# A hybrid attention and state-space layer on one core: a planner's rule for GpSimd, and another order of the first tiles

## The chip, the core and the metric

The kernel runs on one core of one Trainium2 chip. Its engines work side by side and wait for each other through semaphores: TensorE (PE, with its weight loads PEld), VectorE (DVE), ScalarE (ACT), GpSimd (POOL) and SyncE (SP), which issues most of the DMAs. The metric is device microseconds of one execution, and less is better.

## The reference, cut to what matters

`x` is 1024 tokens by 2048, all in float32. One combined projection gives ten blocks of columns; two mixers work on them, and one output projection with a residual and a LayerNorm ends the layer.

```python
u = jnp.einsum('bsd,de->bse', h, w_in[layer])              # 2048 -> 6752 columns
q, k, v, z_attn, q_idx, k_idx, w_idx, z_ssd, xbc, dt_raw = _split_cols(u, IN_WIDTHS)
# group A: indexer scores  sum_h w_idx * relu(q_idx . k_idx)  with 16 heads, the top 256 admissible
#   keys of each query, softmax attention over them (8 query heads, 2 key heads), times silu(z_attn)
o_attn = _dsa_attention(q, k, v, q_idx, k_idx, w_idx) * jax.nn.silu(z_attn)
# group B: causal conv of 4 taps and silu on xbc, chunked state-space scan in 4 groups,
#   gated RMSNorm with silu(z_ssd)
o_ssd = _ssd_mixer(xbc, z_ssd, dt_raw, conv_w[layer], conv_b[layer], ...)
mixed = jnp.concatenate([o_attn, o_ssd], axis=-1)
sub = jnp.einsum('bse,ed->bsd', mixed, w_out[layer])
h = _layer_norm(DEEPNORM_ALPHA * h + sub, ln_g[layer], ln_b[layer])
```

## The kernel before, in words

**Projection.** The tokens are worked on in two halves (`h` = 0 and 1) of 512. The columns are cut into 53 tiles of 128 (`ORDER`): `qi` are the eight tiles of indexer queries, `misc` holds indexer keys, indexer weights and dt, `xbc` and `zs` feed the state-space mixer, `k`, `v`, `q`, `z` the attention. A tile needs all 16 blocks of 128 rows of the weights (`KT` = 16); these come in two pieces (`u` = 0 and 1) of 128x1024 floats, 512 KB each. Every float32 operand is split into a high and a low part of type fp32r: ScalarE copies the high part (`wh` from `wr`, `xh` from the raw tokens), and VectorE or GpSimd subtracts it from the raw value to get the low part (`wl`, `xl`). One block then takes three matmuls: `wh` with `xh`, `wh` with `xl`, `wl` with `xh` (`emit_t`). In half 0 a `qi` tile uses only the upper 256 of the 512 tokens, since the lower 256 have no more admissible keys than the top 256.

**Output projection.** 64 more weight pieces (`O`) follow in the same stream and the same split, with four row blocks of tokens each; LayerNorm ends it.

**What sets the order.** The program is written out by a planner while it is built. `Flow` keeps a list of tasks (generators such as `t_qi`, `t_xbc`, `t_ssd`, `t_attn`, `t_topk`), each of which says what it needs; `Sim` holds a model of every engine's clock, and `pump` emits a task's next step when the model says that its inputs are there. Between the tasks the main loop of `run` emits the matmuls of the stream, four steps (`q`) of two blocks a piece; weights are loaded up to eight pieces ahead and split two ahead (`WAHEAD`). On the chip each engine runs its own instructions in the order in which they were emitted. Because all instructions are recorded by one helper, nearly all carry one line in the profile, L290, and are told apart by the names of their tiles.

**GpSimd or VectorE.** `Sim` has a model of a port that the two engines share (`Port`, `shares_port`): where both want it, one of them waits. `pick` chooses an engine for the low part of a weight piece or of the tokens; everywhere else the engine stands in the code ("V" or "G").

**The opening before.** Nine matmuls on zeros (`warm_up`), then the first weight piece in two DMAs, the upper 256 columns of all 16 token blocks in eight DMAs, and the first four `qi` tiles; `misc` follows as the fifth tile. The lower 256 token columns are loaded and split during the third to seventh piece.

## Time and profile before

| | |
|---|---|
| time, median of 3 runs | 1815.16 us (1812.81 to 1815.38) |
| profiled execution: its own time | 1813.86 us |
| profiled execution: span of the trace | 1812.0 us |
| busy: PE / DVE / ACT / POOL | 98% / 57% / 51% / 26% |
| instructions: PE / DVE / ACT / POOL | 8709 / 1934 / 1571 / 415 |
| granted TensorE clock, mean | 0.994 |

The span runs from the first to the last instruction; the profiled execution's time is 1.86 us longer. Times within the trace are us from the start of the span. A PE that is called busy need not be at its peak: its matmuls overlap, and what counts is the distance from one start to the next.

### The profile page before, as it was taken

The page shows a single profiled execution, that of the slowest core. Times are in us where ns is not written, and L with a number is a line of the kernel's source. Part 1 is how long each engine was busy: PE and PEld are TensorE (multiplying, and loading weights), DVE is VectorE, ACT ScalarE, POOL GpSimd, SP SyncE. Part 2 cuts the span into 40 slices and gives each one's busy share as a digit, 9 for nine tenths or more (in the row PEclk, how much of TensorE's full clock was granted, in tenths as well). Part 3 has the DMA queues.
Part 4 walks back from the last instruction along what each step waited for, and adds up shares of the span by engine and source line. Part 5 has one row for each costly group of instructions (what it writes and reads, how often), then busy time and mean ns, then how long its engine had stood idle before and what let it go on. Part 6 is the DMA issues. An engine that isn't in the chain of part 4 may idle for free. (4 is left out here: it accounts for less than half of the span.)

```text
span 1812.0 us, 24251 instructions
## 1 busy us (share of the span) xinstructions
PE 1768.7 (98%) x8709; PEld 1474.0 (81%) x8709; DVE 1032.4 (57%) x1934; ACT 915.2 (51%) x1571; POOL 464.3 (26%) x415
## 2 busy tenths in 40 slices
PE   9999999999999999999999999999999999999996
PEld 7878888888888878878887888778888888888885
DVE  7855565555325567766755473465546445547435
ACT  6557673433234555566577768773365333431221
POOL 5310231121213133421212132022322122332123
PEclk9999999999999999999999999999999999999998
DMA  8323334333344542222333333333344344558642
GB/s 275 115 82 105 109 111 126 111 128 120 134 146 131 192 137 76 76 67 70 99 105 109 119 111 122 117 122 140 120 155 156 110 144 131 158 173 278 222 163 93
DMA packets 120424, 238.11 MB, mean 131 GB/s; under 512 B 12784, under 2 KB 50928, under 8 KB 120304
## 3 DMA queue, kind: packets, MB, share of 16 engines
q1 hardware_dynamic: 120304, 236.57, 40.2%
q8 instruction: 68, 1.11, 0.2%
q14 instruction: 52, 0.43, 0.1%
HBM read 204.47 MB, written 32.05 MB: 131 GB/s over the span
## 5 line engine op out<-in xcount | busy, mean ns | idle before, releaser
L290 PE MATMUL pj<-xh,wh 128*128 128x512 f32 (+1 forms) x1696 | 665.0, 392 | 1.8 <-ACT xh L290 1.8
L290 PE MATMUL pj<-xh,wl 128*128 128x512 f32 (+1 forms) x1696 | 650.4, 383 | 0.6 <-DVE wl L290 0.6
L290 PE MATMUL pj<-xl,wh 128*128 128x512 f32 (+1 forms) x1696 | 650.0, 383 | 1.0 <-DVE xl L290 0.5
L290 DVE TENSOR_TENSOR wl<-wr,wh 128x1024 fp32r<-128x1024 f32 (+1 forms) x214 | 270.8, 1265 | 504.9 <-ACT wh L290 478.1
L290 ACT ACTIVATE wh<-wr 128x1024 fp32r<-128x1024 f32 (+1 forms) x272 | 283.8, 1045 | 272.9 <-PE pj L290 218.9
L290 PEld LDWEIGHTS pj<-xh,wl 128*128 128x128 f32 x1696 | 320.3, 189 | 64.8 <-DVE wl L290 1.2
L290 PEld LDWEIGHTS pj<-xh,wh 128*128 128x128 f32 x1696 | 320.7, 189 | 62.0 <-issue 2.9
L290 PEld LDWEIGHTS pj<-xl,wh 128*128 128x128 f32 x1696 | 320.9, 189 | 58.4 <-DVE xl L290 0.9
L290 POOL TENSOR_TENSOR u<-u,u 128x512 f32<-128x512 f32 (+8 forms) x164 | 177.1, 1092 | 509.5 <-DVE u L290 317.5
L290 POOL TENSOR_TENSOR wl<-wr,wh 128x1024 fp32r<-128x1024 f32 (+1 forms) x58 | 139.7, 2408 | 370.6 <-ACT wh L290 359.4
L290 PE MATMUL a<-u,u 128*128 128x512 f32 (+3 forms) x840 | 181.2, 342 | 8.9 <-DVE u L290 5.3
L290 PE MATMUL pj<-wh,xh 128*128 128x512 f32 x464 | 183.1, 395 | 0.7 <-ACT u L290 0.7
L290 PE MATMUL pj<-wl,xh 128*128 128x512 f32 x464 | 180.9, 390 | 0.0
L290 PE MATMUL pj<-wh,xl 128*128 128x512 f32 x464 | 180.8, 390 | 0.0
L290 PEld LDWEIGHTS a<-u,u 128*128 128x128 f32 x840 | 137.4, 189 | 40.9 <-DVE u L290 8.4
L290 ACT ACTIVATE u<-s,sm 128x640 bf16<-128x640 int16 (+7 forms) x132 | 130.1, 985 | 32.4 <-DVE sm L290 29.3
L290 ACT ACTIVATE u<-a 128x256 fp32r<-128x256 f32 (+3 forms) x182 | 61.7, 367 | 153.6 <-PE a L290 98.0
L290 ACT ACTIVATE u<-pj 128x512 f32<-128x512 f32 x90 | 53.4, 594 | 146.8 <-PE pj L290 127.4
L290 ACT ACTIVATE a<-a 128x512 f32<-128x512 f32 (+3 forms) x160 | 75.6, 505 | 80.5 <-PE a L290 76.2
L290 PEld LDWEIGHTS pj<-wh,xl 128*128 128x128 f32 x464 | 87.1, 188 | 18.6
L290 PEld LDWEIGHTS pj<-wh,xh 128*128 128x128 f32 x464 | 87.2, 188 | 17.6 <-ACT u L290 1.2
L290 PEld LDWEIGHTS pj<-wl,xh 128*128 128x128 f32 x464 | 87.3, 188 | 16.3
(120 smaller groups left out, 1758.2 us busy)
## 6 DMA issues: line engine op xcount, KB each, us to landing
wr<-wt SPq DMA_DIRECT2D x211, 512.0 KB, 3.3
wr<-wo SPq DMA_DIRECT2D x61, 512.0 KB, 3.7
s<-arow SPq DMA_DIRECT2D x32, 256.0 KB, 4.6
u<-mx SPq DMA_DIRECT2D x32, 256.0 KB, 4.9
u<-xn SPq DMA_DIRECT2D x32, 256.0 KB, 5.6
out<-u SPq DMA_DIRECT2D x32, 256.0 KB, 2.9
u<-arow SPq DMA_DIRECT2D x64, 64.0 KB, 4.3
mx<-u SPq DMA_DIRECT2D x16, 256.0 KB, 2.4
```

Source lines behind the costliest of these rows:

```text
L290: f(*args, **kw)
```

## The change

Three things. The choice between VectorE and GpSimd is made by the planner in more places (`two` calls `pick` where "G" stood in the code: the rope's sine product, the low parts of keys, values, queries and indexer queries, the state-space products), and `pick` has another rule: VectorE takes the operation if the model has it on the port at any time between GpSimd's start and end, and GpSimd takes it only if it would end first. The model's rule on which VectorE operations use the port is changed at small sizes. And the opening is another: `misc` and two `xbc` tiles (512 columns each) come first and take turns, two token blocks each; their first weight pieces come in three parts of 256, 256 and 512 columns; the first part of each is issued by ScalarE, all others by SP; the tokens come in whole blocks of 512 columns. 16 matmuls on zeros stand ahead in place of 9. An unused path (`KEEP`) is removed.

```diff
+FIRST = [("misc", 0), ("xbc", (0, 0)), ("xbc", (0, 1))]
+ORDERS = [[ORDER.index(x) for x in FIRST + [y for y in ORDER if y not in FIRST]],
+          [ORDER.index(x) for x in FIRST[:1] + [y for y in ORDER if y not in FIRST[:1]]]]
...
-        if n < 16 or op in ("max", "match_replace"):
+        if op in ("max", "match_replace"):
             return False
         if op in ("tensor_scalar", "tensor_copy"):
-            return n > 128 and len(sb) == 1 and not in_psum(outs[0])
+            return n >= 128 and len(sb) == 1 and not in_psum(outs[0])
...
-    def pick(self, n, bias=0.0):
-        if any(e[2] == "V" and e[0] > max(self.t, e[3] + 200) for e in self.sim.port.busy):
+    def pick(self, n, *ins):
+        at = self.sim.written(*ins) + Sim.LAT
+        g = max(self.clk["G"], at)
+        end = g + 180 + 2.16 * n
+        if any(e[2] == "V" and e[1] > g and e[0] < end for e in self.sim.port.busy):
             return "V"
-        g = max(self.clk["G"], self.t) + 180 + 2.16 * n
-        v = max(self.clk["V"], self.t) + 145 + 1.042 * n
-        return "G" if g + bias < v else "V"
+        return "G" if end < max(self.clk["V"], at) + 145 + 1.042 * n else "V"
+
+    def two(self, out, a, b, op):
+        self.tt(self.pick(out.free_size(), a, b), out, a, b, op)
...
+            first = len(FIRST) if h == 0 else 0
+            steps = [(t, u) for u in range(2) for t in tiles[:first]]
...
+    def start(self, nf):
...
+        def load(k):
+            if k in (0, 2, 4):
+                c = slice(k * 128, (k + 2 if k < 4 else 8) * 128)
+                for i in range(nf):
+                    (nc.sync if k else nc.scalar).dma_start(*part(i, c))
+            self.x_load(0, k)
...
+        for u in range(2):
+            for q in range(4):
+                k0 = 8 * u + 2 * q
...
+                if u == 0 and q < 3:
+                    chunk(0, q)
+                split(k0)
+                split(k0 + 1)
...
+                for i in range(u * nf, u * nf + nf):
...
+                    fl.pump()
+                    self.emit_t(i, 0, self.stream[i][2], u, q)
...
-        for _ in range(9):
+        for _ in range(16):
             nc.tensor.matmul(b, z[:, 0:128], z[:, 128:640], start=True, stop=True)
...
-        fl.tt("G", tmp, tmp, sin, ALU.mult)
+        fl.two(tmp, tmp, sin, ALU.mult)
...
-        self.sub("G", a2[0:64], x[64:128], f32(a2[64:128]))
+        fl.two(a2[0:64], x[64:128], f32(a2[64:128]), ALU.subtract)
...
-                fl.tt("G", y3, y3, ea[:, k0:, j], ALU.add)
+                fl.two(y3, y3, ea[:, k0:, j], ALU.add)
...
-            fl.tt("G", xs[j], xs[j], zg[j], ALU.mult)
+            fl.two(xs[j], xs[j], zg[j], ALU.mult)
```

What it makes of the instructions, counted over the whole program: VectorE has 2100 in place of 1898 and GpSimd 205 in place of 420. 47 subtractions of a whole weight piece (128x1024) leave GpSimd (56 to 9), and so do 51 products and sums of 128x256, 40 of 128x512, 20 of 32x512, 10 of 64x512 and smaller ones. ScalarE has 59 table loads in place of 47. TensorE has the same projection matmuls, and the seven more on zeros.

**TensorE, the first projection matmuls.** In `pj_53_319` and the like the last number tells tiles of one name apart; `xh_5_114` is the high part of the first token block. Before, behind the nine matmuls on zeros:

```order
L290 MATMUL pj_53_319<-xh_5_114,wh_46_197 128x256
L290 MATMUL pj_53_319<-xl_6_115,wh_46_197 128x256
L290 MATMUL pj_53_319<-xh_5_114,wl_47_198 128x256
L290 MATMUL pj_53_319<-xh_7_116,wh_46_197 128x256
L290 MATMUL pj_53_319<-xl_8_117,wh_46_197 128x256
L290 MATMUL pj_53_319<-xh_7_116,wl_47_198 128x256
```

And now, behind the sixteen (`pj_63_317` is `misc`, `pj_64_324` the first `xbc` tile; the second, `pj_65_331`, follows with the same two token blocks before `misc` goes on with the third):

```order
L291 MATMUL pj_63_317<-xh_12_126,wh_4_118 128x512
L291 MATMUL pj_63_317<-xl_13_127,wh_4_118 128x512
L291 MATMUL pj_63_317<-xh_12_126,wl_5_119 128x512
L291 MATMUL pj_63_317<-xh_14_128,wh_4_118 128x512
L291 MATMUL pj_63_317<-xl_15_129,wh_4_118 128x512
L291 MATMUL pj_63_317<-xh_14_128,wl_5_119 128x512
L291 MATMUL pj_64_324<-xh_12_126,wh_7_121 128x512
L291 MATMUL pj_64_324<-xl_13_127,wh_7_121 128x512
L291 MATMUL pj_64_324<-xh_12_126,wl_8_122 128x512
```

A token block is now used by nine matmuls of 512 columns before the next two are needed, where it was used by three of 256.

**SyncE, the first DMAs** (`wr` and `s_52` are raw weights, `s_4` and `u` raw tokens, the last numbers are the elements moved). Before:

```order
L290 DMA wr_110<-wt 128x512 x2
L290 DMA s_4_113<-xt 128x2x256
L290 DMA s_9_119<-xt 128x2x256
L290 DMA s_14_125<-xt 128x2x256
L290 DMA s_19_131<-xt 128x2x256
L290 DMA wr_137<-wt 128x1024
```

And now; ScalarE has issued the 128x256 parts of `wr_117`, `wr_120` and `wr_123` by itself, as its first three instructions:

```order
L291 DMA u_161<-xt 128x512
L291 DMA u_163<-xt 128x512
L291 DMA wr_117<-wt 128x256
L291 DMA wr_120<-wt 128x256
L291 DMA wr_123<-wt 128x256
L291 DMA u_168<-xt 128x512
L291 DMA u_170<-xt 128x512
L291 DMA wr_117<-wt 128x512
L291 DMA wr_120<-wt 128x512
L291 DMA wr_123<-wt 128x512
```

Before, the first matmul stood behind the two DMAs of a whole weight piece and one of tokens. It now needs one part of a piece and one token block; beside them two more parts and a second token block are under way at once.

**VectorE and GpSimd, one `qi` tile of half 0.** The shuffle and the three products and sums behind it are the rope, `u_749` and `u_748` sum the scores. VectorE before:

```order
L290 TENSOR_TENSOR wl_828<-wr_732,wh_827 128x1024
L290 TENSOR_TENSOR u_808<-u_806,u_808 64x256
L290 TENSOR_TENSOR wl_863<-wr_786,wh_862 128x1024
L290 STREAM_SHUFFLE u_891<-pj_831 128x256
L290 TENSOR_TENSOR pj_831<-pj_831,u_395 128x256
L290 TENSOR_TENSOR wl_898<-wr_848,wh_897 128x1024
L290 TENSOR_TENSOR u_890<-pj_831,u_891 128x256
```

with these on GpSimd in the same stretch:

```order
L290 TENSOR_TENSOR u_807<-u_807,u_396 128x256
L290 MEMSET u_725 64x512
L290 MEMSET u_726 64x512
L290 TENSOR_TENSOR u_809<-u_806,u_809 64x256
L290 TENSOR_TENSOR u_891<-u_891,u_396 128x256
L290 TENSOR_TENSOR wl_949<-wr_901,wh_948 128x1024
```

VectorE now:

```order
L291 TENSOR_TENSOR wl_788<-wr_711,wh_787 128x1024
L291 TENSOR_SCALAR u_749<-a_768,wsc_221 128x512
L291 STREAM_SHUFFLE u_822<-pj_733 128x256
L291 TENSOR_TENSOR pj_733<-pj_733,u_522 128x256
L291 TENSOR_TENSOR u_822<-u_822,u_523 128x256
L291 TENSOR_TENSOR u_821<-pj_733,u_822 128x256
L291 TENSOR_TENSOR wl_831<-wr_740,wh_830 128x1024
L291 SCALAR_TENSOR_TENSOR u_748<-a_779,wsc_221,u_748 128x384
L291 SCALAR_TENSOR_TENSOR u_749<-a_818,wsc_221,u_749 128x512
L291 TENSOR_TENSOR u_823<-u_821,u_823 64x256
L291 TENSOR_TENSOR u_824<-u_821,u_824 64x256
```

The sine product (`u_822<-u_822,u_523`), the second of the two low parts (`u_824`) and every weight piece of this stretch stand on VectorE now; GpSimd has no product, sum or subtraction until the weight pieces of a much later tile.

## Rows read from the trace of the kernel before

**Rows 1.** Busy time of the engines over the whole span, from the first part of the page.

```profile
PE 1768.7 (98%) x8709; PEld 1474.0 (81%) x8709; DVE 1032.4 (57%) x1934; ACT 915.2 (51%) x1571; POOL 464.3 (26%) x415
```

**Rows 2.** The busy time of each engine in eight stretches that follow each other, from the first projection matmul (7.22) to the last matmul (1795.5). Columns: stretch; its length; PE busy (instructions), PEld, DVE, ACT, POOL; granted TensorE clock as a share of full speed; share of the DMA engines; GB/s.

```profile
7.22:40.00 32.78, 31.55 (x215) 29.30 (x216) 28.91 (x39) 21.43 (x43) 19.23 (x18) 0.95 0.92 310
40.00:70.00 30.00, 27.70 (x187) 25.69 (x186) 26.76 (x49) 17.57 (x30) 12.84 (x13) 0.94 0.44 146
70.00:110.00 40.00, 37.72 (x188) 30.44 (x188) 30.27 (x46) 25.66 (x45) 10.64 (x10) 1.00 0.17 57
110.00:660.00 550.00, 548.30 (x2660) 456.24 (x2659) 284.99 (x562) 257.43 (x439) 115.50 (x127) 1.00 0.40 130
660.00:760.00 100.00, 97.27 (x470) 80.35 (x470) 75.23 (x148) 59.32 (x127) 37.23 (x30) 1.00 0.23 71
760.00:1300.00 540.00, 528.75 (x2550) 436.28 (x2549) 316.20 (x588) 349.52 (x578) 132.56 (x111) 1.00 0.35 111
1300.00:1600.00 300.00, 297.93 (x1567) 252.49 (x1566) 157.08 (x364) 134.78 (x254) 76.06 (x61) 1.00 0.42 138
1600.00:1795.50 195.50, 195.49 (x874) 162.02 (x872) 100.19 (x128) 44.11 (x49) 53.76 (x30) 1.00 0.57 191
```

**Rows 3.** What TensorE waited for, summed over the span (us in total, times, longest).

```profile
PE a L290 <- DVE u L290: 5.5, 7, 1.9
PE a L290 <- POOL sm L290: 4.3, 2, 2.4
PE a L290 <- ACT u L290: 4.0, 1, 4.0
```

**Rows 4.** Stretches around the times at which the granted clock was 0.50, columns as in rows 2.

```profile
5.20:8.61 3.41, 1.26 (x7) 0.88 (x7) 1.83 (x4) 2.56 (x8) 1.41 (x2) 1.00 1.03 334
8.61:12.02 3.41, 3.41 (x18) 3.27 (x17) 2.78 (x5) 2.79 (x7) 1.34 (x3) 0.50 1.07 375
66.64:70.05 3.41, 3.41 (x13) 2.82 (x13) 2.53 (x6) 1.67 (x3) 0.00 (x0) 0.50 0.48 154
1148.66:1152.07 3.41, 3.41 (x9) 2.66 (x9) 2.15 (x5) 2.39 (x4) 0.00 (x0) 0.50 0.37 95
```

**Rows 5.** The opening, in order of time, cut to single rows. Columns: start; length; engine; line; operation; out<-in; shapes; count; in brackets the idle time of the engine before it and what ended that.

```profile
1.41 3.97 PE L290 MATMUL a<-s 128*128 128x512 bf16 x9 [1.41 <-POOL s L290]
...
6.05 0.72 ACT L290 ACTIVATE wh<-wr 128x256 fp32r<-128x256 f32 x2 [1.94 <-DMA wr<-wt]
...
7.22 0.38 PE L290 MATMUL pj<-xh,wh 128*128 128x256 f32 x1 [1.84 <-ACT xh L290]
...
7.92 0.38 PE L290 MATMUL pj<-xl,wh 128*128 128x256 f32 x1 [0.31 <-DVE xl L290]
...
9.66 0.41 PE L290 MATMUL pj<-xl,wh 128*128 128x256 f32 x1
9.88 0.41 PE L290 MATMUL pj<-xh,wl 128*128 128x256 f32 x1
...
12.14 0.28 PE L290 MATMUL pj<-xl,wh 128*128 128x256 f32 x1
12.26 0.28 PE L290 MATMUL pj<-xh,wl 128*128 128x256 f32 x1
...
13.13 0.39 PE L290 MATMUL pj<-xl,wh 128*128 128x256 f32 x1 [0.48 <-POOL xl L290]
...
14.42 1.06 ACT L290 ACTIVATE wh<-wr 128x1024 fp32r<-128x1024 f32 x1 [0.58 <-DMA wr<-wt]
```

**Rows 6.** The stretch of the indexer tiles of half 0, cut to five rows of the order of time.

```profile
63.38 2.38 POOL L290 TENSOR_TENSOR wl<-wr,wh 128x1024 fp32r<-128x1024 f32 x1 [1.65 <-ACT wh L290]
...
63.57 2.27 DVE L290 SCALAR_TENSOR_TENSOR sm<-dt,nea 128x64 f32<-128x64 f32 x1
...
66.43 1.53 PE L290 MATMUL a<-u,u 128*128 128x512 f32 x3 [1.95 <-DVE u L290]
...
103.08 1.28 ACT L290 ACT_TABLE_LOAD   x1
...
104.84 0.73 PE L290 MATMUL a<-u,u 128*128 128x512 f32 x2 [1.77 <-DVE u L290]
```

**Rows 7.** Groups of instructions over the whole span, shapes apart: line, engine, operation, out<-in, shapes, count; busy us, mean ns of one; idle time of the engine before them and what ended it.

```profile
L290 DVE TENSOR_TENSOR wl<-wr,wh 128x1024 fp32r<-128x1024 f32 x212 | 269.9, 1273 | 498.8 <-ACT wh L290 472.1 <-PE pj L290 7.0 <-DMA u<-arow 5.7
...
L290 DVE SCALAR_TENSOR_TENSOR pj<-cv,cw,pj 128x512 f32<-128x512 f32 x96 | 72.4, 754 | 8.2 <-ACT pj L290 4.6 <-POOL cv L290 1.3
...
L290 DVE SCALAR_TENSOR_TENSOR u<-a,wsc,u 128x512 f32<-128x512 f32 x15 | 11.2, 750 | 4.0 <-ACT a L290 3.0
...
L290 DVE SCALAR_TENSOR_TENSOR u<-a,wsc,u 128x384 f32<-128x384 f32 x15 | 9.2, 615 | 1.0
...
L290 DVE STREAM_SHUFFLE u<-pj 128x256 f32<-128x256 f32 x8 | 3.6, 450 | 0.0
...
L290 DVE TENSOR_TENSOR u<-pj,u 128x256 f32<-128x256 f32 x8 | 3.3, 417 | 0.4 <-POOL u L290 0.2
...
L290 POOL TENSOR_TENSOR wl<-wr,wh 128x1024 fp32r<-128x1024 f32 x56 | 138.2, 2468 | 366.6 <-ACT wh L290 355.5 <-DVE s L290 11.1
```

**Rows 8.** Half 1, around the longest single wait of TensorE.

```profile
1144.11 1.28 ACT L290 ACT_TABLE_LOAD   x1
...
1147.52 0.66 PE L290 MATMUL a<-c,u 128*128 128x128 f32 x4 [4.05 <-ACT u L290]
```

More of the change, by code (lines that the diff above doesn't have):

```diff
@@ L357, in placed @@
         self.steps += 1
-        self.last = cell
         self.cells.append(cell)
@@ L540, in units @@
         for h in range(2):
-            tiles = list(range(len(ORDER)))
-            if h == 1:
-                tiles.insert(0, tiles.pop(ORDER.index(("misc", 0))))
-            steps = [(t, u) for t in tiles[:-2] for u in range(2)] + [(t, u) for u in range(2) for t in tiles[-2:]]
+            tiles = ORDERS[h]
+            first = len(FIRST) if h == 0 else 0
+            steps = [(t, u) for u in range(2) for t in tiles[:first]]
+            steps += [(t, u) for t in tiles[first:-2] for u in range(2)] + [(t, u) for u in range(2) for t in tiles[-2:]]
             for t, u in steps:
@@ L561, in w_load @@
         raw = fl.new("wr" if fl.slots["wr"] else "s4", [P, 1024])
[L562 to L591 removed]
+        src = self.a["wt" if kind == "T" else "wo"][t, u]
+        if i >= len(FIRST):
+            fl.dma(raw, src)
+        self.wraw[i] = raw
     def w_split(self, i):
         fl = self.fl
[L595 removed]
         raw = self.wraw.pop(i)
         hi = fl.new("wh" if fl.slots["wh"] else "s4", [P, 1024], R)
[L598 to L608 removed]
+        lo = fl.new("wl" if fl.slots["wl"] else "s4", [P, 1024], R)
+        fl.act(hi, raw)
+        fl.two(lo, raw, f32(hi), ALU.subtract)
         fl.free(raw)
[L610 to L611 removed]
         self.w[i] = (hi, lo)
@@ L655, in x_split @@
         fl.act(hi, raw)
-        self.sub(fl.pick(HALF), lo, raw, f32(hi))
+        fl.two(lo, raw, f32(hi), ALU.subtract)
         fl.free(raw)
@@ L700, in run @@
         self.warm_up()
[L701 to L725 removed]
+        nf = len(FIRST)
+        nld = self.start(nf)
+        nsp = self.nsp
+        last_t = ORDERS[0][-1]
         self.fetched = 0
[L727 removed]
+        for i, rows in work[2 * nf:]:
             kind, h, t, u = self.stream[i]
@@ L1246, in t_kv @@
             yield Need("G")
-            self.sub("G", lo, raw, f32(hi))
+            fl.two(lo, raw, f32(hi), ALU.subtract)
             fl.free(raw)
@@ L1280, in t_attn @@
             yield Need("G")
-            self.sub("G", ql, raw, f32(qh))
+            fl.two(ql, raw, f32(qh), ALU.subtract)
             yield Need("", sm=1)
@@ L1530, in t_ssd @@
         yield Need("G")
-        fl.tt("G", zg[0], zg[0], zg[1], ALU.add)
+        fl.two(zg[0], zg[0], zg[1], ALU.add)
         yield Need("P", a=1, sm=1)
```

128 lines of the change are left out of this document (45 added, 83 removed).

## The prediction

> **What bounds the kernel now.** I read the busy times first: TensorE is busy for 98% of the span and every other engine for 57% or less [rows 1]. So what can be won or lost is TensorE's idle time, the time at its half clock, and the two ends. Next I cut the span into stretches and took the length less PE's busy time of each [rows 2]: idle are 1.23 us from 7.22 to 40, 2.30 from 40 to 70, 2.28 from 70 to 110, 1.70 up to 660, 2.73 from 660 to 760, 11.25 from 760 to 1300, 2.07 up to 1600, and 0.01 in the output projection. That is 23.6 us, with 7.22 us ahead of it before the first projection matmul [rows 5]. Then the clock: in three stretches of 3.41 us the granted clock is 0.50, which is 1.2 GHz in place of 2.4, each a little behind an idle gap of PE [rows 4]. In the first, one 256-column matmul starts 0.22 after the last, where it is 0.12 at full clock [rows 5], so one such stretch costs 3.41 x (1 - 0.12/0.22) = 1.5 us. Last, who was waited for: VectorE, a small operation on GpSimd, ScalarE [rows 3], all of them for the short matmuls of the side tasks, hardly ever for the weights. The end behind the last matmul has the same instructions in the same order on VectorE and ScalarE in both programs; I cost it at nothing.
>
> The sum is made against the profiled execution's 1813.86 us; the median is 1.3 us above it. A measurement of this kernel can tell about 0.2% from no change, 3.6 us.
>
> **Term 1, the opening.** Before, nine matmuls on zeros take 3.97 us from 1.41; PE then idles 1.84 and starts at 7.22 [rows 5]. From 8.61 to 12.02 the clock is at half [rows 4]. Now sixteen stand there. The clock was at full from 5.20 on [rows 4], so I take the seven more at full clock, 0.224 each (195.5 us for 874 matmuls in the last stretch [rows 2]): 5.38 + 1.6 = 6.95. The first projection matmul comes no earlier. Its data: before, the first 512 KB had landed by 6.05, and 3072 KB more by 14.42 [rows 5], 367 KB a us. Now the first part of weights, the first token block, and what is under way beside them are 384 to 896 KB, so they land by at most 6.05 + 384/367 = 7.1; a 256-column copy on ScalarE is 0.36 (two in 0.72 [rows 5]), a 512-column one at most twice that. The start is between 6.95 and 7.1 + 0.36 + 0.72 = 8.2. I take 7.2, as before, since not all that is under way has to land. Then PE needs 9 x 2 matmuls of 0.224 for two token blocks and three parts, 4.0 us, and these are 512 + 384 KB, 2.4 us of landing. ScalarE needs 2 x 0.72 + 3 x 0.36 = 2.5 us and VectorE about the same, so from the second step on the data are ahead. Left is the first low part, which VectorE makes after ScalarE's copy: before, this cost 0.31 and 0.48 [rows 5]; I allow 0.5. So: no stretch at half clock, -1.5; idle 0.5 in place of 1.23, -0.7. Term: **-2.2**; bounds -2.5 (start at 6.95) and +0.8 (start at 8.2 and the half clock behind it all the same, -2.2 + 1.0 + 1.5, and 0.5 more for the third part).
>
> On this the Trainium skill (DMA: Bandwidth & Descriptors, "Rules for kernel authors") has a rule against the change: spreading DMAs over several issuers gives no bandwidth, because all run on the same 16 engines and interleave, and only the issue time is saved. By it the three parts of ScalarE's queue would slow the first token block. The 367 KB a us, all from SP's queue, agree that one queue is enough. Its result is the late start, a rival below.
>
> **Term 2, the indexer tiles of half 0.** In the order now, VectorE has this for one `qi` tile: two weight pieces at 1.273, the shuffle at 0.45, three operations of 256 columns at 0.417, two of 64x256 at the same price, and four score sums, two at 0.615 and two at 0.75 [rows 7]: 2.55 + 0.45 + 1.25 + 0.83 + 2.73 = 7.8 us. PE needs 48 x 0.12 + 4 x 0.224 + 4 x 0.168 (384 columns) = 7.3 us. Eight tiles are 62.4 against 58.4. Into the same stretch fall the conv of the two `xbc` tiles, 6 x 0.754 = 4.5, and `misc`, which I price as two ropes, 3.4: 70.3 against 58.4 us. VectorE is then 11.9 us behind, of which the weights' lead of two pieces covers 2 x 2.9, and the last two tiles' scores, 5.5, can be done later. What is left is 0.6 us. Before, VectorE had less in its queue but waited for GpSimd: it was busy 28.91 of 32.78, 26.76 of 30 and 30.27 of 40 us [rows 2], and a 64-element operation took 2.27 us beside a weight piece on GpSimd; PE idled 1.95 just behind it [rows 6]. With the half clock from 66.64 on [rows 4] the stretch from 40 to 110 lost 2.30 + 2.28 + 1.5 = 6.1 us. Now I take 2.0 idle and one stretch at half clock, 3.5: **-2.6**. Bounds: nothing lost, -6.1; the scores not put off, 0.6 + 5.5 idle and one such stretch, 7.6, so +1.5.
>
> **Term 3, the rest of the moved work.** 42 more weight pieces (1.273), 59 operations of 256 columns (0.42) and some 70 of 512 (0.75) are 53 + 25 + 53 = 131 us more on VectorE, 1032 to at most 1163 us of 1812, 64%. What hides it is TensorE's own time: from 110 to 660 VectorE is busy 285 of 550, from 760 to 1300 316 of 540, from 1300 on below 53% [rows 2]. Where the cover is thin is 660 to 760, with 75.2 of 100 [rows 2]; GpSimd's 37.2 there are at the ratio of the two (1273 to 2468 [rows 7]) some 19 more at most, 94 of 100, less what VectorE no longer waits. What is won: waits behind VectorE operations that were held up by GpSimd as the one at 63.57 was [rows 6]. From 110 to 1600 PE lost 17.75 idle and one stretch at half clock, 19.3 us. The two longest kinds of wait there, on a small GpSimd operation and on ScalarE, 4.3 and 4.0 us [rows 3], have other causes; of the remaining 11 us I take a third, an estimate: **-3.5**. Bounds: 0, and -8.
>
> **Term 4, twelve more table loads.** 1.28 us each [rows 6, 8], 15.4 us on ScalarE, busy 915 of 1812 [rows 1]. Of 47 loads two stand right before a wait: 1.28 of the 1.77 at 104.84 [rows 6], and 1.28 of the 4.05 at 1147.52 [rows 8] with the half clock behind it [rows 4], so 2 x 1.28 + 1.5 = 4.1 for 47; twelve more: **+1.0**. Bounds 0 and +5.5, one more wait like the latter.
>
> The Trainium skill (ScalarE: Activation LUTs, "What ACT_TABLE_LOAD costs") puts a drain of 1.38 us on top of each load's 1.28. By that the term would be +1.7; the rows show 1.28 alone, and I keep to them.
>
> **Sum.** -2.2 - 2.6 - 3.5 + 1.0 = -7.3: 1806.6 against the profiled 1813.86, or 1807.9 against the median. I say **1808**.
>
> **The rivals.**
>
> *The opening's gain is taken back (no change).* The indexer tiles move behind three long tiles, and VectorE, alone there, gives +1.5; the waits of the later stretches are only exchanged for others. -2.2 + 1.5 + 0 + 1.0 = 0.3: 1814 to 1816. For it: the idle time from 760 to 1300 is ScalarE's and of small chains, which any new order shuffles. Against: VectorE's long operations under GpSimd go.
>
> *VectorE becomes the bound in half 1's indexer tiles (slower).* Place: the score sums and splits between 660 and 760. It decides once VectorE's own work per tile passes PE's, 100 us here: 94 by the price above, so bunching by a few us is enough; with 10 us too much PE idles some 7 beyond the weights' lead in two or three gaps, two of them with the half clock behind (1.5 each). With the terms of the last rival: 0.3 + 7 + 3 = +10, 1825; at half that depth 1820. Against: 94 counts waits that disappear.
>
> *The first data come late.* Start at 8.2 with the half clock behind it: term 1 is +0.8, the sum -4.3: 1811.
>
> *A table load falls badly.* Term 4 at +5.5 with terms 2 and 3 halved: -2.2 - 1.3 - 1.8 + 5.5 = 0.2, about 1815.
>
> **How the numbers follow.** Forecast 0.48 (1802 to 1811 as its own range), late data 0.09 (1811), no change 0.18, a bad table load 0.08, VectorE as the bound 0.17. Faster is the forecast and late data, 0.57; the same is the no-change case and most of the table load, 0.24; slower is VectorE and the remainder, 0.19. The range leaves out the best bounds together (-2.5 - 6.1 - 8) and the deep end of the slower case: 1798 to 1821.
>
> **What would show each step.** Term 1: no granted clock of 0.50 between 8 and 20 us, the first projection matmul at 7.0 to 7.6, three tiles done near 40. Term 2: PE's idle time from 40 to 110 at 1 to 4 us, and VectorE above 90% there. Term 3: VectorE near 1100 us busy, GpSimd near 200, the means of the weight pieces on VectorE close to 1.23, and idle time from 110 to 1600 near 14. Term 4: 59 loads and no wait over 3 us behind one. The prediction is wrong if the idle time between 40 and 110 exceeds 8 us, or the one from 760 to 1300 stays at 11 or grows.

## The result and the profile after

The changed kernel takes 1795.13 us, median of 4 runs (1792.78 to 1795.58), against 1814.72 (1812.81 to 1815.38) for the kernel before beside it: a ratio of 0.9891, 95% interval 0.9874 to 0.9908. It is faster, by 19.6 us where 7 were forecast. The profiled execution took 1792.78 us with a span of 1791.0.

Busy times from the first part of the page, and the granted clock in 40 slices, answer to [rows 1] and [rows 4].

```profile
PE 1763.0 (98%) x8716; PEld 1471.3 (82%) x8716; DVE 1074.6 (60%) x2136; ACT 926.3 (52%) x1570; POOL 147.9 (8%) x200
...
PEclk9999999999999999999999999999999999999998
```

The stretches of [rows 2], from the first projection matmul (now 6.31) to the last matmul (now 1773.9), with the same columns:

```profile
6.31:40.00 33.69, 33.69 (x153) 27.81 (x152) 21.39 (x34) 18.76 (x32) 0.31 (x2) 1.00 0.84 294
40.00:70.00 30.00, 28.02 (x218) 26.62 (x216) 27.29 (x54) 21.97 (x35) 1.42 (x4) 1.00 0.30 93
70.00:110.00 40.00, 39.72 (x266) 36.45 (x265) 36.87 (x70) 25.94 (x45) 0.00 (x0) 1.00 0.44 143
110.00:660.00 550.00, 547.20 (x2660) 455.17 (x2659) 303.65 (x642) 267.35 (x455) 34.23 (x64) 1.00 0.41 129
660.00:760.00 100.00, 98.78 (x457) 79.54 (x457) 81.30 (x148) 56.73 (x117) 5.68 (x10) 1.00 0.20 64
760.00:1300.00 540.00, 536.79 (x2628) 443.55 (x2627) 334.82 (x699) 362.52 (x606) 42.10 (x55) 1.00 0.35 111
1300.00:1600.00 300.00, 300.00 (x1567) 256.58 (x1566) 165.14 (x353) 132.50 (x243) 38.38 (x33) 1.00 0.45 147
1600.00:1773.90 173.90, 173.90 (x768) 143.66 (x766) 90.98 (x122) 35.30 (x36) 20.18 (x18) 1.00 0.59 194
```

Length less PE's busy time: 0, 1.98, 0.28, 2.80, 1.22, 3.21, 0 and 0 us, together 9.5 against 23.6 before. The largest part went from 760 to 1300, 11.25 to 3.21. What TensorE still waits for ([rows 3] before: 5.5, 4.3 and 4.0):

```profile
PE a L291 <- DVE ddt L291: 2.7, 2, 1.7
PE a L291 <- DVE u L291: 2.4, 4, 1.1
PE a L291 <- POOL s L291: 1.4, 1, 1.4
PE a L291 <- DVE s L291: 1.1, 5, 0.4
...
PE a L291 <- POOL sm L291: 0.3, 1, 0.3
```

The 1.4 on `s` is the start of the program. The wait on the small GpSimd operation is down to 0.3, and the one on ScalarE is gone. The opening, to be read beside [rows 5]:

```profile
1.41 5.26 PE L291 MATMUL a<-s 128*128 128x512 bf16 x16 [1.41 <-POOL s L291]
...
4.39 0.42 ACT L291 ACTIVATE wh<-wr 128x256 fp32r<-128x256 f32 x1 [0.98 <-DMA wr<-wt]
...
6.31 0.58 PE L291 MATMUL pj<-xh,wh 128*128 128x512 f32 x1
```

ScalarE has its first weights at 4.39 and TensorE starts at 6.31 straight from the zeros, with no bracket of idle time. Groups by form, to be read beside [rows 7] (mean ns behind the busy time):

```profile
L291 DVE TENSOR_TENSOR wl<-wr,wh 128x1024 fp32r<-128x1024 f32 x254 | 312.6, 1231 | 442.0 <-ACT wh L291 428.2 <-DMA u<-arow 4.6 <-DMA u<-ri 3.9
...
L291 POOL TENSOR_TENSOR wl<-wr,wh 128x1024 fp32r<-128x1024 f32 x9 | 21.6, 2401 | 44.0 <-ACT wh L291 41.7 <-DVE pj L291 2.2
...
L291 ACT ACT_TABLE_LOAD x59 | 75.7, 1283 | 11.6 <-PE pj L291 5.3 <-DVE sm L291 3.2 <-issue 2.1
```

47 weight pieces left GpSimd, and those on VectorE take 1231 ns where they took 1273.

The last matmul ends 21.6 us earlier (1795.5 to 1773.9): 0.9 by the start, 14.1 by idle time, and 4.6 if each of the three stretches at half clock is priced as in the prediction, at 1.55 us before rounding. These make 19.6; where the other 2 us went stays open. The end behind the last matmul is 0.6 us longer.

### The profile page after: what moved, and what is told of

The parts are those of the page before. It is cut to its first block, busy times and chain, and to the rows that moved or that the text cites. A ratio compares the mean times of both kernels' runs of the same rounds, so it can differ in the third digit from the quotient of the medians.

```text
span 1791.0 us, 24088 instructions
## 1 busy us (share of the span) xinstructions
PE 1763.0 (98%) x8716; PEld 1471.3 (82%) x8716; DVE 1074.6 (60%) x2136; ACT 926.3 (52%) x1570; POOL 147.9 (8%) x200
## 4 chain that ended last, share of the span: by engine, by line
PE 84%; DVE 8%; ACT 5%; issue 2%; DMA 1%; POOL 0%; ACTq 0%; DVEq 0%; POOLq 0%
PE pj L291 70%; PE a L291 10%; PE o L291 4%; DVE u L291 3%; ACT u L291 3%; DVE wl L291 2%; DVE s L291 1%; ACT wh L291 1%; DVE pj L291 1%; DMA wr<-wt 1%; ACT L291 0%; ACT pj L291 0%; ACT s L291 0%; ACT a L291 0%; ACT cv L291 0%
## 5 line engine op out<-in xcount | busy, mean ns | idle before, releaser
L291 PE MATMUL pj<-xh,wh 128*128 128x512 f32 (+1 forms) x1672 | 653.4, 391 | 0.0
L291 PE MATMUL pj<-xh,wl 128*128 128x512 f32 (+1 forms) x1672 | 639.1, 382 | 0.0
L291 PE MATMUL pj<-xl,wh 128*128 128x512 f32 (+1 forms) x1672 | 638.5, 382 | 0.0
L291 DVE TENSOR_TENSOR wl<-wr,wh 128x1024 fp32r<-128x1024 f32 (+1 forms) x263 | 316.8, 1206 | 446.8 <-ACT wh L291 433.0
L291 PEld LDWEIGHTS pj<-xh,wl 128*128 128x128 f32 x1672 | 314.2, 188 | 62.4
L291 PEld LDWEIGHTS pj<-xh,wh 128*128 128x128 f32 x1672 | 314.6, 188 | 58.4 <-issue 2.9
L291 PEld LDWEIGHTS pj<-xl,wh 128*128 128x128 f32 x1672 | 314.8, 188 | 55.7
L291 DVE TENSOR_TENSOR u<-u,u 128x256 f32<-128x256 f32 (+8 forms) x164 | 90.3, 564 | 11.4 <-ACT u L291 10.0
L291 DVE TENSOR_TENSOR u<-a,u 128x256 fp32r<-128x256 f32 (+2 forms) x160 | 64.9, 437 | 35.5 <-ACT u L291 32.1
```

The costliest lines, as they stand in the source:

```text
L291: f(*args, **kw)
```

## The experiments

Theory P: GpSimd's operations hold up VectorE's, and the change took them away. Theory O: the new order of emission happens to be a luckier one. Two more came up on the way, Q (the chains are shorter without GpSimd) and M (the corrected port model makes a better order). "Median" is that of the runs of the kernel named; ratios are against the kernel before on the same chip, with 95% intervals. "Idle 760 to 1300" is the length less PE's busy time of that stretch, as in [rows 2], 11.25 before and 3.21 after.

### The two halves of the change, and no choice at all

`open_only` is the changed kernel with the old choice, port model and fixed GpSimd places.

```diff
+        if n < 16 or op in ("max", "match_replace"):
...
+        if any(e[2] == "V" and e[0] > max(self.t, e[3] + 200) for e in self.sim.port.busy):
             return "V"
...
-        fl.two(tmp, tmp, sin, ALU.mult)
+        fl.tt("G", tmp, tmp, sin, ALU.mult)
```

> The new opening (three long tiles in turns, first weights in parts, 16 matmuls on zeros) with the old rule of choice and GpSimd in all its old places. Theory P (what was lost was VectorE held up by GpSimd): the opening alone is worth the early start and the half clock behind it, 0.9 + 1.5 us, and the 1.2 us of idle up to 40 us; the rest of the idle time stays, so 1808 to 1812, with VectorE's weight pieces still at a mean near 1.27 us. Theory O (a new order of emission, whatever it is, dissolves the old gaps): 1796 to 1805, with GpSimd as busy as before.

`rule_only` is the kernel before with the other part alone, the new choice, the new port model and `two` at all its places: the same lines the other way round.

> The old opening with the new rule of choice at all places and the new port rule of the model. Theory P: most of the gain is here, 1797 to 1804, idle time of TensorE from 110 to 1600 near 7 us in place of 17.8, VectorE's weight pieces at 1.21 us. Theory O: anywhere between 1796 and 1815; then GpSimd's busy time does not tell the result.

`b_all_v` is the kernel before, old port model and old opening, with all these operations on VectorE.

```diff
+    def two(self, out, a, b, op):
+        self.tt("V", out, a, b, op)
...
-        fl.tt("G", tmp, tmp, sin, ALU.mult)
+        fl.two(tmp, tmp, sin, ALU.mult)
...
```

> The old opening, and every product, sum and subtraction that the planner or the code could give to GpSimd outside the opening's fixed places stands on VectorE. Theory P: no choice by a model is needed, only GpSimd off the port: within 3 us of the run with the rule alone. A rival within it (the choice matters, VectorE alone becomes the bound): 5 us or more above the run with the rule alone, with idle time between 40 and 110 and between 660 and 760.

`b_lat85` is the kernel before with one number of the order's model changed, so that the order moves and the engines hardly do.

```diff
-    LAT = 70.0
+    LAT = 85.0
```

> The kernel before with one number of the planner's model changed, the delay from one engine to another (85 ns in place of 70): the same work on the same engines, another order of emission. Theory P: GpSimd still holds VectorE up, so 1808 to 1822, as before give or take. Theory O: the gaps at 965, 1147 and 1208 us are accidents of one order, and this lands up to 12 us lower, near 1803.

| kernel | median us | ratio | idle 760 to 1300 |
|---|---|---|---|
| `open_only` | 1806.50 | 0.9957 (0.9943 to 0.9972) | 10.26 |
| `rule_only` | 1798.74 | 0.9913 (0.9896 to 0.9929) | 3.19 |
| `b_all_v` | 1795.85 | 0.9899 (0.9884 to 0.9913) | 2.93 |
| `b_lat85` | 1812.99 | 0.9995 (0.9986 to 1.0005) | 8.14 |

The stretch in `open_only` and in `rule_only`:

```profile
760.00:1300.00 540.00, 529.74 (x2550) 436.87 (x2549) 313.12 (x596) 348.31 (x578) 129.46 (x108) 0.99 0.33 108
```

```profile
760.00:1300.00 540.00, 536.81 (x2620) 443.21 (x2619) 334.68 (x692) 364.77 (x610) 40.01 (x54) 1.00 0.34 111
```

The opening gives 6.6 us, a time that lies between the two ranges expected, and leaves the middle as it was; choice and model give 14.4 and carry the whole middle. Putting everything on VectorE, without any choice, gives 17.3. Another order of the old kernel gives nothing: P, it seemed, and not O.

### Which operations, and whether the choice is needed

`b_splits_v` has the old choice answer VectorE (it serves the pieces of weights and x alone); `b_fixed_v` puts the eight places fixed on GpSimd on VectorE and leaves the choice.

```diff
     def pick(self, n, bias=0.0):
+        return "V"
```

```diff
-        fl.tt("G", tmp, tmp, sin, ALU.mult)
+        fl.tt("V", tmp, tmp, sin, ALU.mult)
...
```

> The kernel before with one function changed: its old choice, which serves the weight pieces and the pieces of x alone, always answers VectorE. The operations written for GpSimd by hand stay there. Theory L (the long pieces of 2.4 us do the harm, since a VectorE operation beside one lasts until its end): most of the 17 us that all of them on VectorE gave, 1798 to 1801, VectorE's wl mean under 1.21 us. Theory S (the many small operations fixed on GpSimd stand in the chains that TensorE waits for): 1807 to 1811, with the waits of 2 to 4 us on ScalarE and the small GpSimd operation still there.

> The kernel before with the other half of it alone: the eight places written for GpSimd by hand go to VectorE, the old choice for the pieces of weights and x stays. Theory L: 1807 to 1811, since the pieces of 2.4 us still stand beside VectorE. Theory S: 1798 to 1802. If both this and its counterpart give 8 to 10 us, the gain goes by GpSimd's busy time (some 180 us of pieces, some 180 us of fixed operations) and by neither kind.

1807.80 us, ratio 0.9961 (0.9948 to 0.9974), and 1808.07, 0.9961 (0.9946 to 0.9975); idle from 760 to 1300 4.19 and 5.93 us. Neither L nor S: each half gives 7 us; the first leaves 308 us of GpSimd work and the second 330, from 464. The second half is not a clean one: with its eight places gone, the old choice gave GpSimd 80 whole weight pieces, where it had given 56. And in the first, with no whole weight piece on GpSimd, those on VectorE still took 1265 ns in the mean, so shorter GpSimd operations hold them too.

`all_v` is the changed kernel with everything on VectorE; `a_lat85` is the changed kernel with the latency of 85 ns, and `allv_lat85` is both.

```diff
     def two(self, out, a, b, op):
-        self.tt(self.pick(out.free_size(), a, b), out, a, b, op)
+        self.tt("V", out, a, b, op)
...
```

> The changed kernel with its choice taken out: every operation for which it chooses between VectorE and GpSimd goes to VectorE. Theory P (GpSimd's operations hold VectorE up, and that is what the change removed): the nine weight pieces and some forty small operations still on GpSimd cost a little; VectorE's busy time goes from 1075 to about 1098 us, GpSimd's from 148 to about 100, and the time is 1790 to 1795, the choice worth nothing. Rival V (the choice keeps VectorE from being the bound): VectorE is at 81% from 660 to 760 and above 90% from 7 to 110 in the changed kernel; with all of it there PE waits for it, and the time is 1797 to 1803.

> The changed kernel with one constant of its order's model moved: an operation's latency 85 ns in the place of 70, which moves emissions and some engine choices all over the program. Theory P: the gain is in the engines, not in a lucky order; 1793 to 1798. Rival O (this order happens to leave 7 us of waits from 110 to 1600, another one leaves 15 to 20 as the kernel before did): 1802 to 1810.

> Everything on VectorE, and the latency in the order's model 85 ns in the place of 70. If the 3 us between the changed kernel and its two variants (1787.7 against 1791.0 in the span) are luck of the order, this one lies anywhere from 1787 to 1793. If the longer latency orders better in itself, 1784 to 1788, below either edit alone.

1789.29 (ratio 0.9858, 0.9843 to 0.9873), 1788.89 (0.9856, 0.9841 to 0.9870) and 1788.19 us (0.9851, 0.9836 to 0.9866). All three beat both kernels. Of `all_v`, busy times and the two stretches where VectorE was to be short:

```profile
PE 1763.2 (99%) x8716; PEld 1472.6 (82%) x8716; DVE 1095.7 (61%) x2176; ACT 925.4 (52%) x1568; POOL 94.7 (5%) x160
```

```profile
660.00:760.00 100.00, 99.09 (x470) 80.98 (x470) 88.38 (x170) 61.10 (x127) 5.50 (x12) 1.00 0.20 68
760.00:1300.00 540.00, 538.83 (x2643) 446.10 (x2641) 341.47 (x705) 359.60 (x601) 19.66 (x34) 1.00 0.34 113
```

VectorE busy for 88% of 660 to 760 costs TensorE no more than 81% did. So the choice is worth nothing, and rival V is out. `a_lat85` fell outside both expectations, on the fast side: a change of order alone is worth some 6 us in the changed kernel, whose own order is not among the lucky ones. That is a part of O I had thought excluded.

### GpSimd work that nothing waits for

To `all_v`, `allv_sub` adds a subtraction on GpSimd behind each weight split, whose result nothing reads; `allv_set` adds a two-element copy and two fills with zeros in its place; `allv_sub4` adds the subtraction behind every fourth split.

```diff
         fl.free(raw)
...
+        g.tensor_tensor(out=self.junk, in0=f32(hi), in1=f32(hi), op=ALU.subtract)
```

```diff
         fl.free(raw)
...
+        g.tensor_copy(self.junk[:, 0:2], f32(hi)[:, 0:2])
+        for _ in range(2):
+            g.memset(self.junk, 0.0)
```

> The changed kernel with everything on VectorE (1789.3), and behind each of the 137 weight splits a GpSimd subtraction of two copies of the tile's first half into a scratch tile that nothing reads: work beside the kernel's, 137 times about 2.4 us = some 330 us, which no result waits for. Theory P (GpSimd's subtractions hold VectorE's up, wherever they come from): GpSimd goes back to some 430 us, VectorE's weight pieces from a mean of 1.20 to 1.25 us or more, and the time to 1803 to 1815. Rival Q (the gain came from chains that lost a slow link when their operations left GpSimd, and contention costs little): 1788 to 1793.

> The same with other work in the same places: a copy of two elements of the split weights, to hold the place in time, and two fills of the scratch tile with zeros in the place of the subtraction, about 2.2 us which read nothing from SBUF. Theory P in its narrow form (it is reading two SBUF operands on both engines that collides): 1788 to 1793, VectorE's weight pieces at 1.20 us. Theory P in a broad form (any work on GpSimd slows VectorE or the rest): 1800 to 1815, as with the subtraction. Rival Q: 1788 to 1793 here and with the subtraction.

> Everything on VectorE, with the unread GpSimd subtraction behind every fourth weight split alone: 69 times 2.55 us = 175 us (there are 273 splits, not 137 as said of the run with all of them). Theory P, price even per subtraction: a quarter of 107 us, 1814 to 1820. Theory P, price by collisions that pile up: less than in proportion, 1795 to 1805, near the 7 us that came from taking as much GpSimd work off the kernel before. Theory Q: 1788 to 1792.

1896.53 us (ratio 1.0447, 1.0431 to 1.0463), 1796.03 (0.9897, 0.9880 to 0.9913) and 1803.09 (0.9925, 0.9908 to 0.9941), against 1789.29 without. The first two expectations counted 137 splits where there are 273, so the dose was twice what they say; the 107 us of `allv_sub` are far more than twice the 14 to 26 that theory P gave it. `allv_set` lies between the ranges of P's narrow and broad form. Busy times, the group of the weight pieces and the longest waits of `allv_sub`:

```profile
PE 1797.8 (95%) x8716; PEld 1483.5 (78%) x8716; DVE 1314.8 (69%) x2176; ACT 927.5 (49%) x1568; POOL 796.0 (42%) x433
```

```profile
L291 DVE TENSOR_TENSOR wl<-wr,wh 128x1024 fp32r<-128x1024 f32 x263 | 373.0, 1419 | 330.5 <-ACT wh L291 327.0 <-PE a L291 3.0
```

```profile
PE a L291 <- DVE u L291: 25.9, 21, 4.8
PE o L291 <- DVE s L291: 19.3, 9, 5.5
```

And of `allv_set`, busy times and the same group:

```profile
PE 1765.3 (98%) x8716; PEld 1472.3 (82%) x8716; DVE 1112.1 (62%) x2176; ACT 925.7 (52%) x1568; POOL 853.4 (48%) x979
```

```profile
L291 DVE TENSOR_TENSOR wl<-wr,wh 128x1024 fp32r<-128x1024 f32 x263 | 322.1, 1225 | 399.0 <-ACT wh L291 388.3 <-PE pj L291 4.7 <-PE a L291 2.7
```

GpSimd is as busy in the one as in the other, 796 and 853 us. Subtractions that read SBUF make VectorE 219 us busier for the same instructions (1314.8 less 1095.7) and the kernel 107 us slower; fills make it 16 us busier and 7 us slower, where the kernel's own GpSimd operations come late behind the fills (TensorE waits 7.0 us for them and 1.9 in `all_v`). In both variants ScalarE's next split has to wait for GpSimd's added work, 91.7 us over 26 times with the subtractions and 70.2 over 24 with the fills, so that is not the difference. That GpSimd's subtractions hold VectorE up and that this costs time is shown, and Q falls as the whole explanation. The narrow form, that only two operations which both read two SBUF operands collide, is not quite right: the weight pieces are as fast beside fills as without (1225 and 1224 ns), but most of the 16 us are VectorE operations with a single input that the fills held (the last section has the rows). The Trainium skill (SBUF — State Buffer, "Who interferes with whom") says that GpSimd contends with a VectorE instruction of two SBUF inputs when it reads SBUF, not when it only writes; these two runs agree, 1419 against 1225 ns.

Every fourth subtraction, 177 us of them, costs 12 us by the ratios and 14 by the medians: some 0.2 us each, where all 273 cost 0.39 each. So holds pile up. Taking 156 us of pieces off the kernel before (464 to 308) had given 7. That holds which the order does not know of cost more than others would fit this, but is not shown: the operations and their places differ too.

### The corrected port model by itself

The model's change is two lines: it now counts VectorE operations below 16 elements that have two inputs in SBUF, and single-input ones of just 128 elements, as users of the port. No run has one of the two lines without the other. `b_newport` is the kernel before with these alone; `b_newport85` adds the latency of 85 ns; `b_lat100` has the old model and 100 ns; `old_port` and `allv_oldport` put the old model into the changed kernel and into `all_v`.

```diff
-        if n < 16 or op in ("max", "match_replace"):
+        if op in ("max", "match_replace"):
             return False
         if op in ("tensor_scalar", "tensor_copy"):
-            return n > 128 and len(sb) == 1 and not in_psum(outs[0])
+            return n >= 128 and len(sb) == 1 and not in_psum(outs[0])
```

> The kernel before with the corrected model of the port alone; the old choice reads that model, so pieces may change engine, and the order moves. Theory M: 1806 to 1811, waits on the small GpSimd operation gone. Theory E: 1811 to 1817, the long waits elsewhere but as many.

> The kernel before with the corrected port model and the latency of the order's model at 85 ns in the place of 70. Theory M (an order made with the right model keeps TensorE from waiting behind the shared port): again 1802 to 1808, with 760 to 1300 near 3 us idle. Theory O (the 11 us were one lucky order): 1810 to 1817, with some 8 to 11 us idle there.

> The kernel before with the old port model and the latency at 100 ns. Theory M: 1810 to 1817 like the kernel before and its variant at 85 ns (1813.0), since a model that misses the same holds places the same waits elsewhere. Theory O: orders scatter by 10 us, so 1805 to 1820, and a value under 1808 would speak for it.

> The changed kernel with the old model of the shared port (operations under 16 elements, and scalar ones of just 128, taken to need no port); it moves order and some choices. Theory M (the corrected model puts the small sm chains where TensorE does not wait for them, so the waits on the small GpSimd operation come back): 1798 to 1804. Theory E (the engines alone): 1788 to 1796, within what a change of order gives.

> Everything on VectorE and the old model of the port: the order alone moves, a little. Theory M: 1793 to 1800 against 1789.3. Theory E: 1787 to 1792.

| kernel | port model | GpSimd busy us | median us | ratio | idle 760 to 1300 |
|---|---|---|---|---|---|
| `b_lat100` | old | 483.7 | 1809.91 | 0.9974 (0.9964 to 0.9985) | 10.39 |
| `b_newport` | new | 478.9 | 1805.25 | 0.9937 (0.9923 to 0.9952) | 3.06 |
| `b_newport85` | new | 455.7 | 1803.33 | 0.9939 (0.9924 to 0.9953) | 3.78 |
| `old_port` | old | 143.7 | 1798.60 | 0.9902 (0.9887 to 0.9917) | 6.17 |
| `allv_oldport` | old | 95.2 | 1790.82 | 0.9859 (0.9844 to 0.9874) | 2.63 |

`b_newport` is a little below the range that theory M gave it, `b_newport85` within it, `b_lat100` just under the lower end of its own. Of `b_newport`, the stretch, the group and the longest waits:

```profile
760.00:1300.00 540.00, 536.94 (x2605) 443.60 (x2603) 327.95 (x609) 355.87 (x593) 145.26 (x117) 1.00 0.34 111
```

```profile
L290 DVE TENSOR_TENSOR wl<-wr,wh 128x1024 fp32r<-128x1024 f32 x207 | 261.5, 1264 | 481.9 <-ACT wh L290 464.4 <-PE pj L290 7.0 <-DMA wr<-wo 4.4
```

```profile
PE a L290 <- DVE u L290: 5.4, 7, 1.9
PE pj L290 <- ACT xh L290: 2.1, 2, 1.2
PE a L290 <- POOL cv L290: 1.8, 1, 1.8
```

GpSimd does as much as before and VectorE's pieces are held as long (1264 ns against 1273 in [rows 7]), yet the idle time of the middle is gone, and with it the waits of 4.3 and 4.0 us on the small GpSimd operation and on ScalarE [rows 3], of which 0.6 is left. The loss of idle time holds at two latencies, while the old model left 8.1 to 11.3 us there at three latencies and with the other opening. The single waits are no such sign: with the old model at 85 and at 100 ns the wait on ScalarE is gone as well and 2.2 and 1.6 us are left of the other, but new waits have taken their place. The kernel at 100 ns is 5 us faster than before all the same: its idle time in the middle stayed, but the middle has no stretch at half clock. So orders scatter by some 5 us, and M's 11 us stand above that, twice; that these are two orders against three, and that the best of the three is 6.6 us behind `b_newport85`, is all the evidence there is. Where everything is on VectorE and GpSimd has 95 us left, the model hardly matters (1790.82 against 1789.29, as theory E had it).

What the old model missed shows in the trace of the kernel before: a weight piece on GpSimd and a single-input operation of 128 columns on VectorE beside it, and then all 128 of these operations (shortest, median, longest, ns), before and, in the last line, in `b_newport`.

```profile
884.10 2.55 POOL L290 TENSOR_TENSOR wl<-wr,wh 128x1024 fp32r<-128x1024 f32 x1 [6.36 <-ACT wh L290]
...
884.64 2.08 DVE L290 TENSOR_SCALAR s<-s,ac 128x128 f32<-128x128 f32 x1
...
L290 DVE TENSOR_SCALAR s<-s,ac x128: 267/280/2500, 170.5 to 1174.1; 128x128 f32<-128x128 f32 x128
...
L290 DVE TENSOR_SCALAR s<-s,ac x128: 265/279/2500, 172.1 to 1167.8; 128x128 f32<-128x128 f32 x128
```

It takes 0.28 us alone and 2.08 beside the piece, ending with it; the old model gave it no hold at all. The corrected model does not take such holds away: in `b_newport` the longest is 2500 ns as before, and seven of the 128 take over 1 us, where five did. Nor do these holds set the idle time: in `b_lat85`, with the old model, none of the 128 takes over 1 us, and 8.14 us are idle in the middle. In the changed kernel, with little left on GpSimd, the longest is 287 ns. So what the corrected model changes is the order, with a few choices of engine (61 and 53 whole weight pieces on GpSimd at the two latencies, for 56), and not these holds.

In the changed kernel itself the old model costs 2 us by the ratios and 3.5 by the medians (`old_port`), which is within the scatter of orders; the wait on the small GpSimd operation, 0.3 us, did not come back as theory M had it, though the idle time of the middle went from 3.21 to 6.17.

How a hold leads to a wait of TensorE is not shown. The three longest waits of the middle before are 2.40 us at 964.93, 4.05 at 1147.52 and 1.93 at 1208.13. Ahead of the first:

```profile
962.47 1.22 DVE L290 TENSOR_TENSOR wl<-wr,wh 128x1024 fp32r<-128x1024 f32 x1 [2.55 <-ACT wh L290]
...
963.85 1.03 POOL L290 TENSOR_TENSOR sm<-sm,mhalf 128x4 f32<-128x4 f32 x1 [6.02 <-DVE sm L290]
...
964.93 1.16 PE L290 MATMUL a<-c,sm 128*128 128x128 f32 x8 [2.40 <-POOL sm L290]
```

The weight piece has its full speed, and the small operation that GpSimd waits for stands behind it in VectorE's queue. In the 15 us ahead of each of the three, the most that any VectorE operation takes above the shortest of its form is 0.72 us (ahead of the second):

```profile
1139.42 1.14 DVE L290 TENSOR_TENSOR u<-u,cdec 128x256 f32<-128x256 f32 x1
```

So no long hold stands near these waits; they belong to the order in which the operations were emitted. How the model's two lines led away from that order stays open; that they did is shown by the runs alone.

### Fewer matmuls on zeros

`warm9` is the changed kernel with 9 matmuls on zeros in place of 16.

```diff
-        for _ in range(16):
+        for _ in range(9):
```

> The changed kernel with 9 matmuls of zeros at the start in the place of 16. In the changed kernel they run from 1.41 to about 6.3 us, the first projection matmul follows them at 6.31 with no idle between, and its operands were there at 5.35. Theory W (the zeros carry the full clock into the projections): the clock falls to half for one stretch of 3.4 us once TensorE waits for data, +1 to +2 us, 1796 to 1798. Rival E (seven of them only stand in the way): first projection matmul at 5.3 to 5.5, no half clock after it, 1794 to 1795.

1793.87 us, ratio 0.9883 (0.9868 to 0.9897), not to be told from the changed kernel. The opening went as rival E says:

```profile
1.41 4.02 PE L291 MATMUL a<-s 128*128 128x512 bf16 x9 [1.41 <-POOL s L291]
5.54 0.59 PE L291 MATMUL pj<-xh,wh 128*128 128x512 f32 x1
6.27 0.50 PE L291 MATMUL pj<-xl,wh 128*128 128x512 f32 x1
6.60 0.39 PE L291 MATMUL pj<-xh,wl 128*128 128x512 f32 x1
```

It starts 0.77 us earlier, but by the third matmul the lead is 0.37 (6.60 against 6.97), because the second waits for VectorE, and the clock stays full. The seven more zeros are not what removed the half clock of the opening. Ahead of its first projection matmul TensorE now idles 0.11 us (5.43 to 5.54) where it idled 1.84 [rows 5], since its operands are there earlier; whether that alone did it, or the longer matmuls behind it too, no run tells apart.

## Why the prediction was right or wrong

**Direction and bound: right.** TensorE stayed the bound, at 98%, and what was won is idle time and half clock.

**Term 1, the opening: the direction right, the size too small.** -2.2 was said, -2.5 at best; the stretch gave -0.9 (start), -1.2 (idle) and -1.5 (no half clock), -3.6. The start of 6.95 was taken from the end of the zeros; the next matmul starts before that, at 6.31. The first data were earlier than the rate of landing allowed for (first copy at 4.39; the sum had them landed by 7.1, counting from the whole first piece at 6.05, though the trace before has a first weight copy at 3.38 too), and the 0.5 us allowed for VectorE's first low part did not show. The rival of late data is out. By itself `open_only` gives 6.6 us, 3 more than these 3.6; its gains further on are of the size by which orders scatter.

On the issuers of these first parts the Trainium skill's rule (DMA: Bandwidth & Descriptors, "Rules for kernel authors") was cited against the change. With parts on ScalarE's queue and SP's the first copy is at 4.39; no run here has them on one queue, so the rule is neither borne out nor refuted.

**Term 2, the indexer tiles of half 0: right.** -2.6 said, -3.8 measured: 1.98 and 0.28 idle and no half clock in place of 6.1. VectorE is at 91 and 92% there, as said, and is just fast enough.

**Term 3, the rest of the moved work: this step failed.** From 110 to 1600 TensorE lost 19.3 us before and 7.2 after (2.80 + 1.22 + 3.21): -12.1, where the sum has -3.5 and its best bound -8, and where 14 us of idle time were named as the sign. Of the 12.2 us by which the sum is short, 8.6 are this term. Two steps of it are wrong. The first put the waits of 4.3 and 4.0 us on the small GpSimd operation and on ScalarE at nothing, as having other causes, without saying which. The change removed both but for 0.3 us; so did `b_newport`, which changes only the port model, but for 0.6. It is true that no long hold stands ahead of them. But they were waits of one order: the old model's other orders had others in their place, and those made with the corrected model have fewer. The second is what the sum leaves out: the two lines of the port model stood in the change and in no term, as if a better model of the same holds could not move the time. They alone are worth 11 us in the kernel before. The two causes take each other's place and don't add: the model alone gives 11, everything off GpSimd with the old model 17, and the change's choice with the model, which leaves GpSimd 161 us, 14 (`rule_only`). Some 1.5 us of the -12.1 may be luck of the one profile: that of `warm9`, the same kernel with fewer zeros, has a stretch at half clock behind 657 us that the changed kernel's does not have (the last section).

The cover was judged rightly: 60% for VectorE, near 1100 us, the pieces at 1231 ns (1.23 said). From 660 to 760 it is 81.3 of 100, not 94; the prediction had said that 94 counts waits that disappear. The rival with VectorE as the bound did not come, and `all_v` shows that 88 there is harmless too.

**Term 4, the table loads: the count right, the price not seen.** There are 59 loads as said, and no wait over 3 us behind one. But the largest sum of waits that TensorE has left, the 2.7 us on `ddt` in two waits, stands behind loads. The later one:

```profile
655.32 1.28 ACT L291 ACT_TABLE_LOAD   x1
656.61 0.22 ACT L291 ACTIVATE cdec<-a 128x64 f32<-128x64 f32 x1
...
656.87 0.22 DVE L291 TENSOR_TENSOR ddt<-a,ac 128x64 f32<-128x64 f32 x1 [1.93 <-ACT cdec L291]
...
657.15 0.66 PE L291 MATMUL a<-u,u 128*128 128x128 f32 x3 [1.69 <-DVE ddt L291]
```

Before, the waits with a load in their way were 1.20 at 670.33 and 4.05 at 1147.52; now they are 1.04 at 69.61 and 1.69 at 657.15. The wait at 104.84, which the prediction counted too, hung on no load: VectorE, which TensorE waited for there, had worked without a gap since 101.79. So more loads went with less waiting behind them, and no run changes the loads alone: +1.0 is not borne out, and that they are free is not shown either. The Trainium skill (ScalarE: Activation LUTs, "What ACT_TABLE_LOAD costs") adds a drain of 1.38 us to each load. It does not show here: the load starts 0.02 us after the operation ahead of it ends (655.30) and the next one 0.01 us after the load.

**The rival of exchanged waits** had a point: it said that any new order shuffles the idle time from 760 to 1300, and `b_lat85` does just that, with 8.14 us left of it. The two orders made with the corrected model shuffled less back.

## What to carry to other kernels

A wait that the profile puts down to a small operation or to a third engine belongs to one order of the program. Before setting it aside, ask what makes the order: here a change to the planner's model, with as much work on GpSimd as before, removed nearly all of both waits and 8 us of idle time. To find what a model leaves out, look for instructions that take far longer than the shortest of their form (shortest, median and longest of a group show it). Where a program written in a planned order shares a port between two engines, either a plan that knows the operations using the port or doing without the slower engine can help: here each of these removed the same 8 us of idle time, and the second was the simpler and the faster. A new order by itself is worth some 5 us either way, so judge a change of a planner by more than one order.

## What the hardware showed

A GpSimd operation that reads SBUF holds not only VectorE's operations with two inputs. Single-input ones were held too: the one of 128x128 above, 2.08 us in place of 0.28, and in `allv_sub` one of 128x2:

```profile
194.22 1.93 POOL L582 TENSOR_TENSOR junk<-wh 128x1024 bf16<-128x1024 f32 x1 [1.31 <-ACT wh L291]
...
194.31 1.86 DVE L291 TENSOR_SCALAR sm<-sm 128x2 f32<-128x2 f32 x1
```

Four microseconds on, the same operation takes 0.16. The hold lasts until GpSimd's operation ends (at 196.15, and VectorE's at 196.17). Neither model counts an operation of this kind.

Fills held single-input operations too, though they read nothing. In `allv_set` the same operation takes 1.00 us beside a fill of 128x1024, and the longest of the 128 operations above takes 1051 ns, where `all_v` has 289:

```profile
203.57 1.00 DVE L291 TENSOR_SCALAR sm<-sm 128x2 f32<-128x2 f32 x1
...
203.60 1.96 POOL L584 MEMSET junk<- 128x1024 bf16 x2
...
L291 DVE TENSOR_SCALAR s<-s,ac x128: 265/278/1051, 161.1 to 1157.9; 128x128 f32<-128x128 f32 x128
```

These two forms alone make VectorE 10.6 of the 16 us busier (31.6 us against 26.4 for the 128, 17.9 against 12.5 for those of 128x2).

The same gap of TensorE is not always followed by a half clock. In the changed kernel and in `warm9` it idles 1.69 us at 657, before the same instruction; the stretches behind it:

```profile
657.90:661.30 3.40, 3.40 (x19) 2.89 (x18) 2.60 (x10) 1.04 (x3) 0.74 (x1) 1.00 0.24 99
```

```profile
657.71:661.13 3.42, 3.42 (x11) 2.67 (x10) 1.36 (x5) 0.54 (x3) 0.73 (x1) 0.50 0.23 95
```

The first, of the changed kernel, is at full clock with 19 matmuls, the second, of `warm9`, at half with 11. So the same gap cost some 1.5 us in one profile and nothing in the other, and one profile can flatter a kernel: the changed one's profiled execution is the fastest of its four.
